# An encoder trunk on one Trainium2 core: a shorter stretch for preparing weight sums, and sums loaded into the activations' tiles

## The chip, the core and the metric

The kernel runs on one core of a Trainium2 chip. A core has TensorE (matrix multiply; the profile's PE, and PEld for its weight loads), VectorE (DVE), ScalarE (ACT), GpSimd (POOL) and SyncE (SP), whose queue issues nearly all transfers here, and 16 DMA engines that all queues share. The metric is the device time of one launch in microseconds (us); the time of a version is the median over its runs. The profile shows one execution.

## The reference

Two layers over 256 tokens of width 2048, in float32. Layer 0 mixes tokens with a bidirectional mLSTM, layer 1 with a bidirectional gated recurrence (HGRN2); each layer ends with a gated MLP with a convolution of width 3 over the tokens. Every stage has its RMS norm, and a last norm closes the trunk.

```python
for layer in range(DEPTH):
    hn = rmsnorm(h, norm_mix_g[layer])
    h = h + mixer(hn)                          # mLSTM, then HGRN2
    h = h + conv_glu(rmsnorm(h, norm_ffn_g[layer]), ffn_w_up[layer], ffn_conv_w[layer],
                     ffn_conv_b[layer], ffn_w_down[layer])
return rmsnorm(h, final_g)

def conv_glu(hn, w_up, conv_w, conv_b, w_down):
    a, v = jnp.split(hn @ w_up, 2, axis=-1)    # 2048 -> 2 x 5504
    c = conv_b + sum of the neighbours a[t-1], a[t], a[t+1] times conv_w
    return (gelu(c) * v) @ w_down              # 5504 -> 2048
```

The change lies in `conv_glu`, the feed-forward stage, of both layers.

## The kernel before

**Numbers in two parts.** Weights and activations are float32. Each piece of weights is split into a part `wh`, which ScalarE rounds to TensorE's type (L147), and the rest `wl`, which VectorE forms as weights minus `wh` (L148); activations likewise. A product is three matmuls (high by high, high by low, low by high); in the up projection two of them share one matmul of 512 columns (L357), and the third has 256 (L361).

**Stages of the feed-forward.** `ffn` (L1175) cuts the 43 blocks of 128 hidden columns into two parts, of 22 (`FA`) and 21 (`FB`). A part first has its **up chunks**, one for each block: 16 steps over the 2048 inputs, then `done_up` (L1189) makes the gated result on VectorE and ScalarE in a tile of the tag `avc`. Then follow two **pairs**, the down projection for two output column blocks of 512 each: `w0` for the left half of the output and `w1` for the right. So a layer runs: up chunks, two pairs, up chunks, two pairs. The input `x` of the up chunks lies in 16 tiles `xt0` to `xt15` of 512 columns for each partition (`Norm.take`, L404). Both parts read it. The next norm writes the same tiles anew, when the last pair is nearly through.

**Seven products instead of eight.** In a pair, `squares_by_seven` (L225) takes the hidden blocks two at a time, a **couple** (unit `u`), as a 2 x 2 square of matrices. For the couples in `SEVEN` it uses a scheme of Strassen's kind with seven products. For that it needs sums of weights: T1 to T4. T2, T3 and T4 lie in a tile T of 1536 columns. For most couples these sums are worked out in advance and kept in a scratch in DRAM (`tscr`); the few in `FLY` are made in place by `combine` (L202).

**Preparing sums.** `prepare` (L613) is a side job of a part's up chunks. For each of 12 couples it loads 2048 columns (two transfers of 512 KB on SP, L395), does four subtractions on VectorE (L632) and stores two halves to `tscr` (L635, two transfers of 512 KB). Side jobs run on a clock of the code's own: it ticks 0.65 at a time, 16 times in an up chunk, so a chunk is 10.4 units and a part is `nf * 10.4` (228.8 or 218.4). A job's `yield n` means that it isn't taken up again before n units have gone by; it is taken up at a tick. Before the change, the pause at the start is 18 and the period `(nf * 10.4 - 26) / 12`; within a period there are pauses of a half, four of a 24th, and a third. The tiles for this (`praw`) have the tags `wh` and `wl` of the pool `ff`, of two buffers each. The loads are in program order with the loads of up weights on SP (`late`, L394); the stores aren't.

**A pair's weights.** `split_squares` (L187) first waits, in the order of issue, until all that its pair needs has been prepared (`side.until`: what is left of the job is then issued at once). Then, a unit at a time, it loads 1536 columns of weights into a `raw` tile (three buffers, L135), and for a stored couple T into a tile of the tag `avc` (L198; three buffers, `TEMP`, the ones that `done_up` uses as well) and T1 into the rest of `raw` (L199). Each piece of 1024 columns is then split by L147 and L148. Every third piece uses tiles `wh` and `wl` of the pool `ff`. Pieces are fetched three ahead of TensorE (`LOOK`).

**What sets the order.** The queues of the engines work in order. The framework orders instructions for each engine by priority, the order of issue, and a simulated timeline; matmuls of the up chunks, and loads by `late`, are held in program order. A load waits on SP until its tile is free, and what stands behind it waits too.

**The end.** `FinalNorm` (L476) loads the final norm's weights into `xt0` to `xt3` (four tiles of 512 columns) ahead of the first pair of the last layer's second part, and uses `xt4` and `xt5` as work tiles.

Of the kernel before, what the change touches and what calls it, by code (L numbers as in the profile page):

```python
# [8 lines left out]
F32 = mybir.dt.float32  # L9
F32R = mybir.dt.float32r  # L10
# [5 lines left out]
P = 128  # L16
T = 256
D = 2048
KT = D // P
# [33 lines left out]
SPLIT = (0, 2, 5), (0, 2, 5)  # L53
END = 3
# [12 lines left out]
def trunk_kernel(ctx, tc, xT, x_d, fg_d, pp_d, cst_d, w_gate, w_first, w_aq, w_ak, w_av, w_ao, w_aout, w_ao2,  # L67
# [119 lines left out]
    def split_squares(ch, parts):  # L187

        units, raws, kept = (ch.nk + 1) // 2, {}, {}
        side.until(lambda: all(ch.waits))  # L190

        def raw(u):
            if u not in raws and u < units:
                n = 1536 if u in ch.stored else min(2048, 1024 * ch.nk - 2048 * u)
                raws[u] = load_raw(ch.src, 2048 * u, 2048 * u + n)
                if u in ch.stored:
                    kept[u] = temporary(ch.pool, "T")
                    nc.sync.dma_start(kept[u], ch.stored[u][:, 0:1536])  # L198
                    nc.sync.dma_start(raws[u][:, 1536:2048], ch.stored[u][:, 1536:2048])  # L199
            return raws.get(u)  # L200

        def combine(u):  # L202
            r, T = raw(u), temporary(ch.pool, "T")
            B11, B22, B21, B12 = (r[:, j * 512:(j + 1) * 512] for j in range(4))
            T2, T3, T4 = (T[:, j * 512:(j + 1) * 512] for j in range(3))
            for x, y, out in ((B12, B22, T3), (B12, B11, B12), (B22, B12, T2), (B21, T2, T4)):
                dve.tensor_tensor(out, x, y, ALU.subtract)
            kept[u] = T

        for u in range(units):  # L210
# [4 lines left out]
            if u in ch.seven:  # L215
                yield *parts(kept[u][:, 0:1024], 1024, more=ch.pool), 1
            if 2 * u + 1 < ch.nk:
                yield *parts(r[:, 1024:2048], 1024, more=ch.pool), 1
            if u in ch.seven:
                yield *parts(kept[u][:, 1024:1536], 512, more=ch.pool), 1  # L220
# [177 lines left out]
    class Norm:  # L398

        def __init__(self, gname, goff):  # L400
            self.g, self.o = gname, goff
            self.xs, self.rc_, self.R_ = [None] * KT, None, None

        def take(self, k, src, g=None, *pin):  # L404
            self.xs[k] = keep.tile([P, 2 * T], F32R, tag=f"xt{k}", name=f"xt{k}")
# [70 lines left out]
    class FinalNorm:  # L476
# [6 lines left out]
        def load(self):  # L483
            self.g = [keep.tile([P, 512], F32, tag=f"xt{c}", name=f"fg{c}") for c in range(4)]
# [20 lines left out]
        def half(self, ps, t):  # L505
# [5 lines left out]
            last = keep.tile([P, 512], F32, tag=f"xt{4 + t}", name="fl")  # L511
# [63 lines left out]
    def pair(src, nk, c0, x, sums, norm, seven):  # L575
# [34 lines left out]
        ch.stored, ch.waits, ch.pool, ch.ends, ch.rest = {}, (), None, False, False  # L610
# [564 lines left out]
    def ffn(layer, norm, nxt):  # L1175
# [40 lines left out]
        for part, (f0, nf) in enumerate(((0, FA), (FA, FB))):  # L1216
# [3 lines left out]
            def prep(todo=todo, finished=finished, nf=nf):  # L1220
                if not pairs[0].pool:
# [3 lines left out]
                                  todo, 18.0, (nf * 10.4 - 26.0) / len(todo), finished, late, True))  # L1225
# [6 lines left out]
            def two(src, c0, norm, seven, fly, shares, GT=GT, SX=SX, nf=nf):  # L1232
                ch = pair(src, nf, c0, lambda k: GT[k], lambda u: SX[u], norm, seven)
                ch.waits, left = [], [u for u in seven if u not in fly]
# [148 lines left out]
```

## Time and profile before

| | us |
|---|---|
| median of three runs | 2368.85 |
| the three runs | 2365.73, 2370.08, 2368.85 |
| the profiled execution | 2366.48 |
| its span, first to last instruction | 2364.5 |
| TensorE busy | 2354.1 |
| VectorE busy | 1993.5 |
| ScalarE busy | 1470.0 |

The feed-forward stages lie at these times in the profiled execution: layer 0 has up chunks from 388.7 to 634.3, pairs to 742.3, up chunks to 975.2 and pairs to 1080; layer 1 has up chunks from 1663.7 to 1909.4, pairs to 2017.5, up chunks to 2250.4 and pairs to 2356. The mean granted clock of TensorE is 0.999. Rows of the profile name an instruction by its line (L148), engine, operation and tiles (out<-in); "idle before" is time in which the engine stood still ahead of it, and the arrow names what ended that. A window row gives the stretch, its length, the busy time of every engine with the number of instructions, the clock, the DMA engines' share, and GB/s.

### The profile page before, as it was taken

Reading aid. Unit: us, or ns where it says so; the run is one execution under the profiler, and the core shown is the slowest. Engines: PE = TensorE matmul, PEld = TensorE weight load, DVE = VectorE, ACT = ScalarE, POOL = GpSimd, SP = SyncE. Lnnn points to the kernel's source line nnn. Section 1 sums busy time; section 2 is a strip of 40 time slices with the busy share of each in tenths; the row PEclk is TensorE's granted clock in tenths of the full one; section 3 lists DMA queues with packets and bytes.
Section 4 is the critical chain, followed back from the end, with each engine's and each line's share of the span. In section 5 each row is a group of like instructions: output and inputs, shape, how many; then the busy total and the mean of one; then the engine's idle time right before and its main releaser. Section 6 shows DMA issues by size and latency. Waiting matters only on the chain. (4 is left out here: it accounts for less than half of the span.)

```text
span 2364.5 us, 38407 instructions
## 1 busy us (share of the span) xinstructions
PE 2354.1 (100%) x14545; PEld 2016.2 (85%) x14545; DVE 1993.5 (84%) x3087; ACT 1470.0 (62%) x2340; POOL 196.5 (8%) x244
## 2 busy tenths in 40 slices
PE   9999999999999999999999999999999999999998
PEld 8888888888888888888888888888888888888887
DVE  7777687888998898897888888778789889888888
ACT  7655456555665555676777777776555567455565
POOL 0100000000000000000232322220000000000000
PEclk9999999999999999999999999999999999999999
DMA  8776656888888878996556665646788888888896
GB/s 303 239 248 242 213 195 211 295 282 292 313 321 327 306 282 292 330 334 230 208 203 223 212 225 204 214 169 228 270 300 289 289 321 335 295 287 302 309 351 221
DMA packets 122266, 632.97 MB, mean 268 GB/s; under 512 B 13776, under 2 KB 14928, under 8 KB 77664
## 3 DMA queue, kind: packets, MB, share of 16 engines
q1 hardware_dynamic: 120384, 626.51, 75.0%
q0 software_dynamic: 1120, 3.21, 0.8%
q8 instruction: 114, 1.87, 0.3%
q10 hardware_dynamic: 576, 0.79, 0.1%
q14 instruction: 72, 0.59, 0.1%
HBM read 562.24 MB, written 68.22 MB: 267 GB/s over the span
## 5 line engine op out<-in xcount | busy, mean ns | idle before, releaser
L357 PE MATMUL mm<-xt,wh 128*128 128x512 f32 x3776 | 1312.0, 394 | 0.0
L148 DVE TENSOR_TENSOR wl<-raw,wh 128x1024 fp32r<-128x1024 f32 (+1 forms) x844 | 1037.3, 1234 | 222.6 <-ACT wh L147 214.5
L147 ACT CAST wh<-raw 128x1024 fp32r<-128x1024 f32 (+1 forms) x844 | 875.3, 1042 | 513.0 <-PE mm L357 305.8
L361 PE MATMUL mm<-xt,wl 128*128 128x256 f32 x3776 | 1043.5, 278 | 0.0
L357 PEld LDWEIGHTS mm<-xt,wh 128*128 128x128 f32 x3776 | 705.6, 188 | 160.6 <-issue 0.4
L361 PEld LDWEIGHTS mm<-xt,wl 128*128 128x128 f32 x3776 | 709.4, 188 | 4.5
L373 PE MATMUL mm<-wh,xt 128*128 128x512 f32 x1024 | 324.4, 392 | 0.6 <-ACT wh L147 0.5
L236 PE MATMUL pc<-wh,g 128*128 128x512 f32 (+1 forms) x716 | 243.2, 388 | 0.3 <-ACT wh L147 0.2
L373 PEld LDWEIGHTS mm<-wh,xt 128*128 128x128 f32 x1024 | 191.2, 188 | 40.0 <-ACT wh L147 1.1
L632 DVE TENSOR_TENSOR praw<-praw 128x512 f32<-128x512 f32 x252 | 174.1, 691 | 44.7 <-DMA praw<-in_w_d 29.0
L373 PE MATMUL mm<-wl,xt 128*128 128x512 f32 x512 | 199.7, 391 | 0.0
L236 PEld LDWEIGHTS pc<-wh,g 128*128 128x128 f32 x716 | 134.1, 188 | 29.0 <-ACT wh L147 1.5
L236 PE MATMUL mm<-wh,sx 128*128 128x512 f32 x432 | 153.4, 389 | 0.0
L148 DVE TENSOR_TENSOR wl<-T,wh 128x1024 fp32r<-128x1024 f32 (+1 forms) x144 | 135.9, 955 | 13.3 <-ACT wh L147 8.9
L147 ACT CAST wh<-T 128x1024 fp32r<-128x1024 f32 (+1 forms) x144 | 118.6, 835 | 44.7 <-DMA T<-tscr 18.2
L236 PE MATMUL pc<-wl,g 128*128 128x512 f32 (+1 forms) x358 | 138.8, 388 | 0.0
L591 POOL TENSOR_TENSOR hm<-hm,u 128x512 f32<-128x512 f32 x10 | 14.8, 1481 | 1223.8 <-DVE u L590 1223.8
L373 PEld LDWEIGHTS mm<-wl,xt 128*128 128x128 f32 x512 | 96.2, 188 | 18.6
L1071 DVE TENSOR_TENSOR QK<-QK,G 128x256 f32<-128x256 f32 x224 | 104.6, 515 | 6.2 <-ACT kq L1050 5.9
L1195 ACT COPY avc<-mm 128x256 f32<-128x256 f32 x172 | 64.0, 372 | 63.9 <-PE mm L361 63.6
L1050 ACT COPY kq<-QK 128x512 f32<-128x512 f32 x112 | 74.5, 669 | 37.3 <-DVE QK L1071 29.5
L236 PEld LDWEIGHTS mm<-wh,sx 128*128 128x128 f32 x432 | 81.0, 188 | 16.9 <-ACT wh L147 0.2
(246 smaller groups left out, 2263.1 us busy)
## 6 DMA issues: line engine op xcount, KB each, us to landing
raw<-in_w_up SPq DMA_DIRECT2D x172, 1024.0 KB, 6.1
tscr<-praw SPq DMA_DIRECT2D x126, 512.0 KB, 6.7
praw<-in_w_d SPq DMA_DIRECT2D x120, 512.0 KB, 6.8
raw<-in_w_bq SPq DMA_DIRECT2D x48, 1024.0 KB, 5.0
T<-tscr SPq DMA_DIRECT2D x63, 768.0 KB, 7.6
raw<-in_w_d SPq DMA_DIRECT2D x60, 768.0 KB, 6.0
raw<-in_w_ao SPq DMA_DIRECT2D x24, 1024.0 KB, 4.8
raw<-in_w_d SPq DMA_DIRECT2D x24, 1024.0 KB, 7.7
```

The source lines that it names most:

```text
L147: pin(act.copy(wh[:, :m], r))
L148: pin(dve.tensor_tensor(wl[:, :m], r, wh[:, :m].bitcast(F32), ALU.subtract))
L236: pin(pe.matmul(ps, a, b, start=bank not in begun, stop=stop and i == 2))
L357: hold(pe.matmul(ps[f], wh[:, c:c + P], x, start=k + kk == 0, stop=False))
L361: hold(pe.matmul(ps[f][:, 0:T], wl[:, c:c + P], x[:, 0:T], start=False, stop=k + kk == ch.nk - 1))
L373: pe.matmul(ps[t], x[:, a + t * P:a + (t + 1) * P], w[:, c], start=st and i == 0, stop=sp and i == 2)
L591: pool.tensor_tensor(part(1, 0), part(1, 0), u, ALU.add)
L632: dve.tensor_tensor(out, x, y, ALU.subtract)
L1050: act.copy(m, blocks(QK, h))
L1071: dve.tensor_tensor(two[:, j], two[:, j], by[:, j], ALU.mult)
L1195: act.copy(z, p[:, T:2 * T])
```

## The change

- The period of `prepare` in a part's up chunks becomes `(nf * 10.4 - 60) / 12` instead of `(nf * 10.4 - 26) / 12`. The number of couples and their instructions stay.
- In the pairs of each layer's second part, the couples 2, 3 and 4 get their T not in a tile of the tag `avc` but in tiles of `x`: T2 and T3 (1024 columns) in one tile, T4 (512 columns) in half of another. `LENT` gives for each couple the tile, the other tile and its half. A stored couple's T comes then in two transfers (512 KB and 256 KB) instead of one of 768 KB.
- For that the 16 tiles of `x` are joined by twos into eight (`xt0` to `xt7`) of 1024 columns. The final norm's weights lie in two such tiles, its work tile in a third.

```diff
--- before.py
+++ after.py
@@ -51,6 +51,7 @@
 FLY = (2,), (5,), (2,), ()
 FIRST = 6
 SPLIT = (0, 2, 5), (0, 2, 5)
+LENT = {2: (3, 4, 0), 3: (5, 4, 1), 4: (6, 7, 0)}
 END = 3
 SCRATCH = 4096
 SEVEN_MIX = (2, 4, 6)
@@ -186,26 +187,36 @@
 
     def split_squares(ch, parts):
 
-        units, raws, kept = (ch.nk + 1) // 2, {}, {}
+        units, raws, kept, halves = (ch.nk + 1) // 2, {}, {}, {}
         side.until(lambda: all(ch.waits))
+
+        def place(u):
+            if u not in ch.lent:
+                T = temporary(ch.pool, "T")
+                return T[:, 0:1024], T[:, 1024:1536], T
+            i, j, h = ch.lent[u]
+            if j not in halves:
+                halves[j] = keep.tile([P, 1024], F32, tag=f"xt{j}", name="T")
+            return keep.tile([P, 1024], F32, tag=f"xt{i}", name="T"), halves[j][:, h * 512:(h + 1) * 512], None
 
         def raw(u):
             if u not in raws and u < units:
                 n = 1536 if u in ch.stored else min(2048, 1024 * ch.nk - 2048 * u)
                 raws[u] = load_raw(ch.src, 2048 * u, 2048 * u + n)
                 if u in ch.stored:
-                    kept[u] = temporary(ch.pool, "T")
-                    nc.sync.dma_start(kept[u], ch.stored[u][:, 0:1536])
+                    kept[u] = place(u)
+                    for T, a, b in [(kept[u][2], 0, 1536)] if kept[u][2] else zip(kept[u], (0, 1024), (1024, 1536)):
+                        nc.sync.dma_start(T, ch.stored[u][:, a:b])
                     nc.sync.dma_start(raws[u][:, 1536:2048], ch.stored[u][:, 1536:2048])
             return raws.get(u)
 
         def combine(u):
-            r, T = raw(u), temporary(ch.pool, "T")
+            r, (T, T4, _) = raw(u), place(u)
             B11, B22, B21, B12 = (r[:, j * 512:(j + 1) * 512] for j in range(4))
-            T2, T3, T4 = (T[:, j * 512:(j + 1) * 512] for j in range(3))
+            T2, T3 = (T[:, j * 512:(j + 1) * 512] for j in range(2))
             for x, y, out in ((B12, B22, T3), (B12, B11, B12), (B22, B12, T2), (B21, T2, T4)):
                 dve.tensor_tensor(out, x, y, ALU.subtract)
-            kept[u] = T
+            kept[u] = T, T4
 
         for u in range(units):
             r = raw(u)
@@ -213,11 +224,11 @@
             if u + 1 in ch.seven and u + 1 not in ch.stored:
                 combine(u + 1)
             if u in ch.seven:
-                yield *parts(kept[u][:, 0:1024], 1024, more=ch.pool), 1
+                yield *parts(kept[u][0], 1024, more=ch.pool), 1
             if 2 * u + 1 < ch.nk:
                 yield *parts(r[:, 1024:2048], 1024, more=ch.pool), 1
             if u in ch.seven:
-                yield *parts(kept[u][:, 1024:1536], 512, more=ch.pool), 1
+                yield *parts(kept[u][1], 512, more=ch.pool), 1
 
     def banks():
         return [psm.tile([P, 512], F32, tag="mm", name="mm") for _ in range(2)]
@@ -399,10 +410,12 @@
 
         def __init__(self, gname, goff):
             self.g, self.o = gname, goff
-            self.xs, self.rc_, self.R_ = [None] * KT, None, None
+            self.xs, self.two, self.rc_, self.R_ = [None] * KT, {}, None, None
 
         def take(self, k, src, g=None, *pin):
-            self.xs[k] = keep.tile([P, 2 * T], F32R, tag=f"xt{k}", name=f"xt{k}")
+            if k // 2 not in self.two:
+                self.two[k // 2] = keep.tile([P, 4 * T], F32R, tag=f"xt{k // 2}", name=f"xt{k // 2}")
+            self.xs[k] = self.two[k // 2][:, k % 2 * 2 * T:(k % 2 + 1) * 2 * T]
             split(self.xs[k], src, col(self.g, self.o + k) if g is None else g, *pin)
 
         def squares(self, c, pin=lambda ins: ins):
@@ -481,7 +494,9 @@
             self.rc = small[:, 8:10]
 
         def load(self):
-            self.g = [keep.tile([P, 512], F32, tag=f"xt{c}", name=f"fg{c}") for c in range(4)]
+            g = [keep.tile([P, 1024], F32, tag=f"xt{c}", name=f"fg{c}") for c in range(3)]
+            self.g = [g[c // 2][:, c % 2 * 512:(c % 2 + 1) * 512] for c in range(4)]
+            self.last = g[2]
             for c in range(4):
                 pool.dma_start(self.g[c], fg_d[:, c * 512:(c + 1) * 512].broadcast_to([P, 512]))
 
@@ -508,7 +523,7 @@
             dve.tensor_tensor(hm[:, t, 1024:1536], hm[:, t, 1024:1536], ps[0], ALU.add)
             square(hm[:, t, 1024:1536], ss[:, 2:3])
             dve.tensor_scalar(rc, ss[:, 2:3], 1.0 / D, rc, ALU.mult, ALU.add)
-            last = keep.tile([P, 512], F32, tag=f"xt{4 + t}", name="fl")
+            last = self.last[:, 512 * t:512 * t + 512]
             h = hm[:, t, 1536:2048]
             dve.tensor_tensor(h, h, ps[1], ALU.add)
             m = 256 if t else 512
@@ -607,7 +622,7 @@
 
         ch = Chunk("st", src, nk, x, done)
         ch.mid, ch.seven, ch.sums = mid, seven, sums
-        ch.stored, ch.waits, ch.pool, ch.ends, ch.rest = {}, (), None, False, False
+        ch.stored, ch.waits, ch.pool, ch.ends, ch.rest, ch.lent = {}, (), None, False, False, {}
         return ch
 
     def prepare(tiles, todo, first, period, finished, start, ahead):
@@ -1222,7 +1237,7 @@
                     begin()
                 side.push(prepare(lambda i: [box["mp"].tile([P, 1024], F32, tag=("wh", "wl")[i % 2], bufs=MORE, name="praw")
                                              for _ in range(2)],
-                                  todo, 18.0, (nf * 10.4 - 26.0) / len(todo), finished, late, True))
+                                  todo, 18.0, (nf * 10.4 - 60.0) / len(todo), finished, late, True))
 
             for i in range(nf):
                 chunks.append(Chunk("fm", w_up[layer, f0 + i], KT, norm.x, done_up(f0 + i, i, GT, SX, SEVEN[layer][part]),
@@ -1231,6 +1246,8 @@
                                     fixed=part + i > 0))
             def two(src, c0, norm, seven, fly, shares, GT=GT, SX=SX, nf=nf):
                 ch = pair(src, nf, c0, lambda k: GT[k], lambda u: SX[u], norm, seven)
+                if part:
+                    ch.lent = LENT
                 ch.waits, left = [], [u for u in seven if u not in fly]
                 for n, (todo, finished) in zip(shares, [early[layer]] + lists):
                     for u in left[:n]:
```

## Prediction

> **What bounds the kernel now.** I read the page's engine table first, then a window for each of the four up stretches and the four stretches of pairs, then what the weight loads of TensorE (PEld) waited for, and last the instructions around the longest wait.
>
> ```profile
> PE 2354.1 (100%) x14545; PEld 2016.2 (85%) x14545; DVE 1993.5 (84%) x3087; ACT 1470.0 (62%) x2340; POOL 196.5 (8%) x244
> ```
>
> ```profile
> 388.70:634.30 245.60, 245.60 (x1422) 214.86 (x1421) 213.91 (x349) 141.22 (x223) 0.70 (x1) 1.00 0.85 294
> 634.30:742.30 108.00, 107.93 (x477) 89.01 (x476) 99.39 (x112) 73.08 (x86) 3.54 (x2) 1.00 0.86 320
> 742.30:975.20 232.90, 232.90 (x1346) 203.68 (x1345) 202.47 (x324) 128.30 (x200) 3.53 (x2) 1.00 0.85 301
> 975.20:1080.00 104.80, 104.80 (x471) 86.79 (x470) 97.93 (x111) 74.53 (x96) 7.01 (x4) 1.00 0.82 299
> 1663.70:1909.40 245.70, 245.70 (x1422) 214.85 (x1422) 211.32 (x345) 139.90 (x221) 0.70 (x1) 1.00 0.84 292
> 1909.40:2017.50 108.10, 107.88 (x476) 88.86 (x475) 102.59 (x117) 73.13 (x87) 3.71 (x3) 1.00 0.88 325
> 2017.50:2250.40 232.90, 232.90 (x1346) 203.68 (x1345) 202.44 (x317) 127.17 (x198) 5.63 (x6) 1.00 0.86 302
> 2250.40:2356.00 105.60, 105.07 (x475) 86.76 (x475) 92.61 (x109) 69.84 (x89) 7.58 (x5) 1.00 0.78 290
> ```
>
> The columns are the stretch and its length, the busy time of PE, PEld, DVE, ACT and POOL, the granted clock, the DMA share and GB/s. Odd rows are the up chunks of one part, even rows its two pairs. TensorE is busy through all eight: 1382.78 of 1383.60 us. That alone doesn't exclude slow matmuls, so the pace is read too. The two steady stretches of up chunks while couples are being prepared give 200.00 / 1156 = 173.0 ns and 185.00 / 1069 = 173.1 ns between matmuls:
>
> ```profile
> 412.00:612.00 200.00, 200.00 (x1156) 174.90 (x1155) 175.34 (x288) 112.33 (x179) 0.00 (x0) 1.00 0.84 290
> 612.00:634.30 22.30, 22.30 (x131) 19.52 (x130) 20.76 (x34) 14.27 (x22) 0.00 (x0) 1.00 1.01 369
> 765.00:950.00 185.00, 185.00 (x1069) 161.81 (x1068) 159.49 (x261) 103.28 (x164) 0.00 (x0) 1.00 0.84 297
> 950.00:975.20 25.20, 25.20 (x147) 22.03 (x147) 23.47 (x39) 14.04 (x22) 0.00 (x0) 1.00 0.95 337
> 2250.40:2303.00 52.60, 52.07 (x229) 42.34 (x229) 43.64 (x49) 36.28 (x44) 4.45 (x2) 1.00 0.95 360
> ```
>
> No matmul is added or removed, so the floor stays. What the change can win is the time in which TensorE waits in the pairs. All waits of the weight loads there, first in the first part's pairs (630 to 742 us), then in the third's (1905 to 2020), then in the fourth's (2245 to 2357); in the second's there is none (us in total, times, longest):
>
> ```profile
> PEld pc L236 <- ACT wh L147: 0.5, 1, 0.5
> ...
> PEld pc L236 <- ACT wh L147: 0.7, 1, 0.7
> PEld mm L236 <- ACT wh L147: 0.2, 1, 0.2
> ...
> PEld mm L236 <- DVE wl L148: 1.0, 1, 1.0
> PEld pc L236 <- ACT wh L147: 0.4, 1, 0.4
> PEld mm L236 <- ACT wh L147: 0.2, 1, 0.2
> ```
>
> Together 3.0 us. The most that can be won in the changed stages is **3.0 us**, 0.13% of the time; 0.2% (4.7 us), about what a measurement of this kernel can tell from no change, isn't there to be had in these waits.
>
> The longest of them lies 10 us into the last part's first pair:
>
> ```profile
> 2255.05 0.33 SPq L135 DMA_DIRECT2D raw<-in_w_d  x1
> 2255.43 0.43 SPq L198 DMA_DIRECT2D T<-tscr  x1
> ...
> 2260.31 0.39 PE L236 MATMUL pc<-wh,g 128*128 128x512 f32 x1
> ...
> 2260.54 0.49 PE L236 MATMUL mm<-wh,g 128*128 128x512 f32 x1
> 2260.86 0.40 PE L236 MATMUL pc<-wh,g 128*128 128x512 f32 x1
> 2261.34 1.05 ACT L147 CAST wh<-T 128x1024 fp32r<-128x1024 f32 x1 [0.56 <-DMA T<-tscr]
> ...
> 2261.79 0.50 PE L236 MATMUL mm<-wl,g 128*128 128x512 f32 x1 [0.53 <-DVE wl L148]
> 2262.13 0.40 PE L236 MATMUL mm<-wh,g 128*128 128x512 f32 x1
> ```
>
> Undisturbed starts lie 0.23 us apart (2260.31 to 2260.54). From 2260.86 to 2261.79 it is 0.93, a loss of 0.70; the steps before and after it (0.32 and 0.34) lose 0.1 each. A few matmuls on, the next wait (0.38 us of PEld) is the last 0.2. I put this knot at **1.1 us**. Its sums T were asked for at 2255.43 and taken up at 2261.34. They were asked for late, because T has to have one of three buffers that the up chunks' results (avc) hold, and the last chunks' results are still being made then.
>
> **The change part by part.**
>
> *The shorter stretch.* The rows of L632 give the cost of a couple and when it is done:
>
> ```profile
> L632 DVE TENSOR_TENSOR praw<-praw 128x512 f32<-128x512 f32 x40 | 27.4, 685 | 3.9 <-issue 2.9 <-DMA praw<-in_w_d 0.9
> L632 DVE TENSOR_TENSOR praw<-praw x48: 680/684/694, 406.5 to 623.5; 128x512 f32<-128x512 f32 x48
> L632 DVE TENSOR_TENSOR praw<-praw x48: 679/683/695, 758.3 to 964.0; 128x512 f32<-128x512 f32 x48
> ```
>
> The first row is the stretch 412 to 612: 40 subtractions, so 10 couples in 200 us, 20 us each, 2.74 us of VectorE each. The code's period is (228.8 - 26) / 12 = 16.9 of its own time units, but every one of its six pauses is rounded up to ticks of 0.65: 8.45 + 4 x 1.3 + 5.85 = 19.5, and 12 of these and the first 18 make 252, more than the 228.8 that the part has. So before, the last two couples were not paced at all but were issued at once when the first pair asked for its weights; the window 612 to 634.3 shows it as a DMA share of 1.01. After: 14.07 becomes 7.15 + 4 x 0.65 + 5.2 = 14.95; 12 of them and 18.2 are 197.6, which is 31 units or three up chunks ahead of the pairs, not four (for the second part 14.3, 190 of 218.4, again under three). One unit is 245.6 / 228.8 = 1.073 us, so a couple comes every 16.0 us instead of 20, in the second part every 15.3.
>
> What each instruction of the moved step costs: 48 subtractions a part, unchanged in number, at 685 ns. Without them VectorE is busy (175.34 - 27.4) / 200 = 0.74; with one couple in 16.0 us 0.91 instead of 0.88, in the second part about 0.92. That hides behind TensorE as it does now: in the unpaced bursts VectorE ran at 20.76 of 22.30 and 23.47 of 25.20 us (0.93) and TensorE didn't wait in either. 24 loads and 24 stores a part, on SP's queue: 4 x 512 KB a couple, 2.1 MB, is 105 GB/s at 20 us, 131 at 16.0 and 137 at 15.3. So the up chunks go from 290 to 316 GB/s and from 297 to about 327, by the share 0.84 to about 0.92. Transfers in this window:
>
> ```profile
> raw<-in_w_up SPq DMA_DIRECT2D x36, 1024.0 KB, 6.0
> tscr<-praw SPq DMA_DIRECT2D x20, 512.0 KB, 6.4
> praw<-in_w_d SPq DMA_DIRECT2D x20, 512.0 KB, 7.0
> ```
>
> A raw tile lasts 245.6 / 44 = 5.6 us of TensorE and there are three, so a new one has two such times, 11 us, to land; it takes 6.0. The loads of couples stand in program order ahead of raw loads on SP, and wait for the stores of the couple two before, whose 6.4 us fit into the 12 units between them. I cost it at 0; the ends are -0.5 (below) and +20 (first rival). What is freed: no couples' traffic in the last three up chunks, when the pairs' first loads are issued, and no unpaced burst on VectorE ahead of the last chunk's results. Of the waits in the first and third part (0.5 and 0.9 us, ends 0 and all 1.4 gone) I count none as won. Where the third part's is, a piece waits for T although the couples had been subtracted 30 us before (last start 1899.7):
>
> ```profile
> L632 DVE TENSOR_TENSOR praw<-praw x48: 679/684/693, 1681.5 to 1899.7; 128x512 f32<-128x512 f32 x48
> ...
> 1929.28 1.05 ACT L147 CAST wh<-T 128x1024 fp32r<-128x1024 f32 x1 [3.36 <-DMA T<-tscr]
> ```
>
> *The lent tiles.* In both pairs of each second part, T2 and T3 of couples 2, 3 and 4 go to tiles of x, T4 to half of another. All are stored ones: 12 loads of 768 KB become 12 of 512 and 12 of 256 KB. The added 12 issues hold SP 0.33 us each (the raw row at 2255.05), 1 us a pair, spread over 52 us. x's tiles are read last by the last up chunk, the first of them at half of it: about 2250.4 - 5.6 = 2244.8, the last at 2250.4. T of couple 2 may so be asked for up to 9 us earlier than 2255.43, and nothing that stands behind it on SP is held longer than now: the raw load ahead of it waited to 2255.05 anyway. The 1.1 us knot goes; next in line are couple 5 and later, which then find all three avc buffers free. Value **-1.1**, ends -1.6 (all PEld waits of that part) and 0.
>
> By the Trainium skill, "DMA: Bandwidth & Descriptors", section Bandwidth / Measured, transfers should be batched to 1 MiB or more, which speaks against cutting one into two. Its fit of 2.0 us a transfer beside the bytes gives, as an estimate from that page, 12 x 2.0 = 24 us more DMA time, 2392 us if all of it were exposed; that a small transfer costs nearly as much as a large one the trace confirms (6.8 and 7.6 us, in a rival below).
>
> *x in eight tiles instead of sixteen, and the final norm's rows in halves of two of these.* No instruction changes, and x's tiles were always written in twos. A false wait between the two halves would show at a norm's start; bounds 0 and 4 norms x 0.5 us (one split by ACT is 0.51 us):
>
> ```profile
> 4.53 0.51 ACT L379 ACTIVATE xt<-gx 128x256 fp32r<-128x256 f32 x1 [1.58 <-DMA gx<-in_xT]
> ```
>
> I take 0, since the second half is written right behind the first, before the matmuls are issued.
>
> *Sum.* The profiled execution took 2366.48 us (span 2364.5 and 2.0 around it); 2366.48 - 1.1 = 2365.4. The three runs' median is 2.37 us above that execution. I forecast for the median: 2368.85 - 1.1 = **2367.7 us**, no change by 0.2%.
>
> **The rivals.**
>
> *Denser transfers starve the up chunks (slower).* Place: the 180 us in which couples are now prepared, four times. Up chunks with couples ran at 290 to 302 GB/s so far; nobody has asked 316 to 327 of them for 180 us. TensorE has up to three pieces ready, 3 x 245.6 / 88 = 8.4 us. If the stretch carried only 300 of 322 GB/s, it would end 180 x 22 / 300 = 13 us late, 4.8 beyond what is ready; four times, 19 us: 2387 us. It decides below about 322 x 180 / 189 = 307 GB/s. Against it: the last row of the windows above, 360 GB/s for 52.6 us with 0.5 us of waiting, and 369 GB/s with none. Chance 0.14.
>
> By the Trainium skill, the same page, section "Where 436 GB/s comes from", transfers between HBM and SBUF are held to about 358 GB/s by the HBM side. The trace has gone beyond it (369), and the demand here lies below either.
>
> *The cut transfers land late (slower).* A 256 KB load needs almost as long as a 768 KB one when the pairs begin:
>
> ```profile
> T<-tscr SPq DMA_DIRECT2D x3, 768.0 KB, 7.6
> raw<-tscr SPq DMA_DIRECT2D x4, 256.0 KB, 6.8
> ```
>
> If two halves took turns they would need up to 14 us, 6 more, and one such delay in each of four pairs is 24 us less the 9 us head start of two of them, about +6 to +15: 2374 to 2383. Against it: they overlap on the same 16 engines, and T4 is needed last in its unit. Chance 0.04.
>
> *It doesn't do what it says.* SP keeps T of couple 2 behind the raw load that waits to 2255.05, so the head start isn't used, or another piece is late instead: 2368.9. Chance 0.25, and the same verdict as mine.
>
> *More is won than the profile shows.* The three runs lie up to 3.6 us above the profiled one (2370.08). If that is made of longer waits of the same kind, and the change removes them with all 3.0 us, the median falls to 2368.85 - 2.4 - 3.0 = 2363.5. Chance 0.12.
>
> **How the numbers follow.** My forecast holds 0.45, the change without effect 0.25: no change 0.70. Slower 0.14 + 0.04 = 0.18, faster 0.12. The likeliest case alone reaches from 2365.0 to 2370.5, by the runs' own spread. To leave out no more than 2 in 10, the range takes in the gain of the last rival and the mild end of the slower ones: 2363.3 to 2374.
>
> **What would show it.** Right: L632 ends some 25 us ahead of each first pair; the window ahead of the pairs loses its DMA share of 1.01 and 0.95; T for couples 2 to 4 is asked for before the second parts' pairs begin, and no wait is left near 2261; 173 ns between matmuls in the up chunks. Wrong: waits of ACT for raw<-in_w_up, which aren't in this profile, weight loads waiting on L357, or VectorE above 0.95 between two up chunks.

## The result and the profile after

| | median, us | runs | lowest to highest |
|---|---|---|---|
| before | 2366.95 | 8 | 2365.26 to 2370.08 |
| after | 2376.49 | 8 | 2370.28 to 2379.09 |

The ratio is **1.0033, 95% interval 1.0024 to 1.0042**: slower by a third of a per cent (the medians themselves lie 9.5 us apart, 0.40%). The forecast was no change, at 2367.7 us. The profiled execution of the changed kernel took 2377.22 us, its span 2375.2 us, 10.7 more than the span of before. Lines after the change stand 11 to 15 lower down in the code: L148 and L149 split the weights, L247 is the pairs' product, L368 and L372 are the up chunks' two matmuls, L647 is the couples' subtraction, L209 loads T.

What TensorE's weight loads waited for, over the whole run of the changed kernel (us in total, times, longest):

```profile
PEld mm L372 <- DVE wl L149: 4.1, 3, 1.8
PEld pc L247 <- DVE wl L149: 2.1, 1, 2.1
PEld mm L247 <- ACT wh L148: 1.9, 2, 1.3
PEld pc L247 <- ACT wh L148: 1.4, 3, 0.6
...
PEld mm L247 <- DVE wl L149: 1.1, 2, 0.8
```

The first row is new: 4.1 us in the up chunks, which had none. The pairs (L247) have 6.5 us where they had 3.0. Of these, 5.2 lie in the fourth part. Together that is 7.6 us more than before. Another 1.6 us follow from a lower clock, shown below, so 9.2 of the 10.7 us are accounted for by these rows. Counted from matmul to matmul, the up chunks of the first and the third part take 1.1 and 3.8 us longer than before, the fourth part's pairs with the end 5.1, and all the rest 0.7.

**The up chunks.** The longest of the three waits is this one, in layer 1's first part (timeline of the changed kernel):

```profile
1859.03 0.69 DVE L647 TENSOR_TENSOR praw<-praw 128x512 f32<-128x512 f32 x1 [3.88 <-DMA praw<-in_w_d]
...
1859.63 0.48 DVE L1217 SCALAR_TENSOR_TENSOR avc<-avc,pp 128x255 f32<-128x255 f32 x1
...
1860.03 0.68 DVE L647 TENSOR_TENSOR praw<-praw 128x512 f32<-128x512 f32 x1
1860.20 0.42 ACT L1218 ACTIVATE avc<-avc 128x256 f32<-128x256 f32 x1 [5.01 <-DVE avc L1217]
1860.63 1.22 DVE L149 TENSOR_TENSOR wl<-raw,wh 128x1024 fp32r<-128x1024 f32 x1
...
1861.90 0.39 PE L372 MATMUL mm<-xt,wl 128*128 128x256 f32 x1 [1.49 <-DVE wl L149]
```

VectorE stands still for 3.88 us before a subtraction whose couple hasn't landed. It works in order, so the last chunk's result (L1217) and the next piece of weights (L149) wait behind it, and TensorE waits for that piece. The couple itself is wanted by nobody for 50 us. How short the lead of such a load is can be seen in layer 0's first part, first after, then before:

```profile
570.84 1.36 SPq L406 DMA_DIRECT2D praw<-in_w_d  x2
...
580.53 0.69 DVE L647 TENSOR_TENSOR praw<-praw 128x512 f32<-128x512 f32 x1 [3.40 <-DMA praw<-in_w_d]
```

```profile
598.61 0.80 SPq L395 DMA_DIRECT2D praw<-in_w_d  x2
...
606.15 0.69 DVE L632 TENSOR_TENSOR praw<-praw 128x512 f32<-128x512 f32 x1
```

Before, VectorE came to the subtraction 7.5 us after the load was issued and found it just landed. After, it stood free 6.3 us after the issue and waited the other 3.4. Over the whole run the median time of a praw load to land rose from 6.8 to 7.7 us. VectorE waited for such loads before, too; the whole-run rows are, before and after:

```profile
DVE praw L632 <- DMA praw<-in_w_d: 29.0, 22, 3.4
```

```profile
DVE praw L647 <- DMA praw<-in_w_d: 40.7, 27, 3.9
```

The transfers themselves went as worked out. In the stretch with couples the share is 0.88 at 310 GB/s (0.92 and 316 had been estimated), and ScalarE's waits for up weights, of which there were none, come to 1.5 us (three, the longest 0.9) and lie at 596, 864 and 1837, not where TensorE waits.

```profile
412.00:588.00 176.00, 175.18 (x1011) 153.00 (x1010) 152.53 (x252) 94.59 (x153) 0.00 (x0) 1.00 0.88 310
588.00:636.00 48.00, 48.00 (x279) 42.30 (x278) 43.18 (x70) 30.86 (x49) 0.00 (x0) 1.00 0.76 259
2300.00:2303.20 3.20, 3.20 (x8) 2.53 (x9) 3.20 (x4) 2.37 (x3) 1.55 (x1) 0.50 0.47 136
```

The second row is the quiet time ahead of the pairs that the shorter stretch leaves (couples end at 586.1; 1.01 had been the share here). The third row belongs to the next point.

**The fourth part's pairs.** These start at about 2256 in the changed kernel, and the knot of 1.1 us is gone. New waits come at 2285 and 2297. The last of them, in the timeline:

```profile
2298.61 2.35 DVE L149 TENSOR_TENSOR wl<-raw,wh 128x1024 fp32r<-128x1024 f32 x2
2299.43 2.00 ACT L148 CAST wh<-raw 128x1024 fp32r<-128x1024 f32 x2 [1.96 <-DMA raw<-in_w_d]
...
2299.89 0.76 PE L247 MATMUL pc<-wl,g 128*128 128x512 f32 x1 [1.62 <-DVE wl L149]
2300.45 0.63 PE L247 MATMUL pc<-wh,g 128*128 128x512 f32 x1
```

Now it is `raw`, the weights themselves, that is late. The transfers issued from 2243 to 2300, most of the first pair:

```profile
T<-tscr SPq DMA_DIRECT2D x7, 768.0 KB, 9.2
raw<-in_w_d SPq DMA_DIRECT2D x6, 768.0 KB, 10.0
T<-tscr SPq DMA_DIRECT2D x6, 512.0 KB, 11.4
```

A pair has three lent couples, so three transfers of 512 KB. Six were issued: the second pair's lent sums (3 x 768 KB, 2.4 MB) were fetched during the first, which runs to about 2313. The raw loads take 10.0 us to land; before, seven of them in this place took 6.8. The queue on SP has filled up as well. Its waits from 2250 to 2285 are:

```profile
SPq L209 <- DMA T<-tscr: 6.4, 8, 1.6
SPq L209 <- DMA raw<-in_w_d: 4.0, 2, 2.3
SPq L136 <- DVE wl L149: 2.8, 3, 1.8
SPq L209 <- DMA raw<-tscr: 2.5, 2, 1.3
SPq L136 <- DMA T<-tscr: 2.4, 2, 1.5
```

Issues wait there for the landing of earlier transfers: from 2255.99 to 2282.04, each of 19 issues in a row comes within 0.12 us of the landing of the transfer that SP had issued eight before. Raw loads (L136) stand behind sums that aren't needed for 30 us. In the kernel before, SP waited in this place only for tiles that VectorE was still reading or writing.

After the wait of 2 us the matmuls run at half pace: the window 2300 to 2303.2 above has a granted clock of 0.50. The half clock lasts from 2299.95 to 2303.36, and the eight matmuls in it start about 427 ns apart instead of 227, which is the 1.6 us more.

### The profile page after: what moved, and what is told of

It is laid out like the page before. It is cut to its first block, busy times and chain, and to the rows that moved or that the text cites. A ratio compares the mean times of both kernels' runs of the same rounds, so it can differ in the third digit from the quotient of the medians.

```text
span 2375.2 us, 38403 instructions
## 1 busy us (share of the span) xinstructions
PE 2358.8 (99%) x14545; PEld 2018.3 (85%) x14545; DVE 1990.2 (84%) x3087; ACT 1470.5 (62%) x2340; POOL 196.5 (8%) x244
## 5 line engine op out<-in xcount | busy, mean ns | idle before, releaser
L368 PE MATMUL mm<-xt,wh 128*128 128x512 f32 x3776 | 1313.6, 394 | 0.0
L149 DVE TENSOR_TENSOR wl<-raw,wh 128x1024 fp32r<-128x1024 f32 (+1 forms) x844 | 1037.7, 1235 | 217.0 <-ACT wh L148 211.1
L148 ACT CAST wh<-raw 128x1024 fp32r<-128x1024 f32 (+1 forms) x844 | 875.7, 1043 | 494.0 <-PE mm L368 279.5
L372 PE MATMUL mm<-xt,wl 128*128 128x256 f32 x3776 | 1045.1, 278 | 3.1 <-DVE wl L149 3.1
L368 PEld LDWEIGHTS mm<-xt,wh 128*128 128x128 f32 x3776 | 705.6, 188 | 160.9 <-issue 0.4
L372 PEld LDWEIGHTS mm<-xt,wl 128*128 128x128 f32 x3776 | 709.7, 188 | 8.6 <-DVE wl L149 4.1
L247 PE MATMUL pc<-wh,g 128*128 128x512 f32 (+1 forms) x716 | 244.4, 390 | 0.2 <-ACT wh L148 0.2
L647 DVE TENSOR_TENSOR praw<-praw 128x512 f32<-128x512 f32 x252 | 174.2, 691 | 56.7 <-DMA praw<-in_w_d 40.7
L247 PEld LDWEIGHTS pc<-wh,g 128*128 128x128 f32 x716 | 134.6, 189 | 29.0 <-ACT wh L148 1.4
L247 PE MATMUL mm<-wh,sx 128*128 128x512 f32 x432 | 153.4, 389 | 0.2 <-ACT wh L148 0.2
L149 DVE TENSOR_TENSOR wl<-T,wh 128x1024 fp32r<-128x1024 f32 (+1 forms) x144 | 136.3, 960 | 13.9 <-ACT wh L148 13.3
L148 ACT CAST wh<-T 128x1024 fp32r<-128x1024 f32 (+1 forms) x144 | 118.3, 834 | 43.5 <-PE pc L247 16.9
L247 PE MATMUL pc<-wl,g 128*128 128x512 f32 (+1 forms) x358 | 139.7, 390 | 1.6 <-DVE wl L149 1.6
L247 PEld LDWEIGHTS mm<-wh,sx 128*128 128x128 f32 x432 | 81.0, 188 | 17.4 <-ACT wh L148 0.7
```

Of the source, the lines that this page charges most:

```text
L148: pin(act.copy(wh[:, :m], r))
L149: pin(dve.tensor_tensor(wl[:, :m], r, wh[:, :m].bitcast(F32), ALU.subtract))
L247: pin(pe.matmul(ps, a, b, start=bank not in begun, stop=stop and i == 2))
L368: hold(pe.matmul(ps[f], wh[:, c:c + P], x, start=k + kk == 0, stop=False))
L372: hold(pe.matmul(ps[f][:, 0:T], wl[:, c:c + P], x[:, 0:T], start=False, stop=k + kk == ch.nk - 1))
```

## The experiments

Two theories stood from here on. **Mine:** two separate causes, the subtractions that wait in VectorE's queue for a late couple, and the second pair's lent sums ahead of the first pair's weights. **Rivals:** the denser traffic as such; the transfers cut in two; the first pair's lent transfers.

| run | us | before beside it | ratio, 95% interval |
|---|---|---|---|
| e1 shorter period alone | 2369.81 | 2367.93 | 1.0006 (0.9997 to 1.0015) |
| e2 lent tiles, old period | 2371.35 | 2367.93 | 1.0014 (1.0005 to 1.0023) |
| e3 shorter period, lent in first pairs | 2368.60 | 2367.93 | 1.0002 (0.9993 to 1.0011) |
| e4 all T cut in two | 2367.27 | 2367.93 | 0.9996 (0.9987 to 1.0005) |
| e5 couples' loads on GpSimd's queue | 2377.83 | 2367.19 | 1.0047 (1.0035 to 1.0060) |
| e6 the same, lent in first pairs | 2376.23 | 2367.19 | 1.0041 (1.0028 to 1.0055) |
| e7 shorter period, lent in second pairs | 2377.44 | 2367.19 | 1.0044 (1.0031 to 1.0056) |
| e8 old period, lent in first pairs | 2364.85 | 2367.19 | 0.9988 (0.9980 to 0.9997) |
| e9 as e2, pairs' loads in program order | 2372.55 | 2367.25 | 1.0021 (1.0012 to 1.0030) |
| e10 as e3, couples' loads earlier | 2365.61 | 2367.25 | 0.9993 (0.9984 to 1.0001) |
| e11 changed kernel with both repairs | 2369.14 | 2367.25 | 1.0007 (0.9998 to 1.0016) |
| e12 x in eight tiles alone | 2368.50 | 2367.25 | 1.0006 (0.9997 to 1.0014) |

### e1: the shorter period alone

```diff
 # the kernel before
-                                  todo, 18.0, (nf * 10.4 - 26.0) / len(todo), finished, late, True))
+                                  todo, 18.0, (nf * 10.4 - 60.0) / len(todo), finished, late, True))
```

> The kernel before with the shorter period alone. My theory has two separate causes, and this run holds only the first: in the up chunks a couple's subtraction stands in VectorE's queue before its load has landed, and the wl pieces behind it wait with it. Then VectorE's wait for praw should rise from 29.0 us to about 40 us, TensorE should wait for wl in the up chunks (about 4 us in all, at two to four places, as in the changed kernel: 1.0, 1.1 and 1.8 us), and the time should be about 2 to 4 us above before. The pairs of the fourth part should show no wait above 1.2 us. Rival 1, the transfers cut in two or lent are the only cause: no time lost, 0 us. Rival 2, the up weights themselves come late because of the denser traffic: the same loss, but ScalarE waits for raw<-in_w_up.

Measured 1.0006. What TensorE waited for, beside the start:

```profile
PE mm L361 <- DVE wl L148: 2.1, 3, 1.0
```

Three waits in the up chunks, at the places where the changed kernel has them (near 582, 1843 and 1861). ScalarE's waits for up weights are two, 1.4 us in all, and not at these places. The wait for praw rose to 54.3 us. The interval takes in no change, so it is the trace that shows this cause and not the time: the up chunks of the first and the third part take 1.7 and 2.4 us longer than before.

In the fourth part's pairs (2245 to 2365) no weight load waits at all. The knot of 1.1 us is gone with the shorter stretch alone, though nothing is lent here, and the pairs with the end take 1.2 us less than before. That is part of why the time shows less than the up chunks lose.

### e2: the lent tiles alone

```diff
 # the changed kernel
-                                  todo, 18.0, (nf * 10.4 - 60.0) / len(todo), finished, late, True))
+                                  todo, 18.0, (nf * 10.4 - 26.0) / len(todo), finished, late, True))
```

> The changed kernel with the old period. It holds the lent tiles and not the shorter stretch. My theory: the fourth part's pairs still lose 4 to 6 us, since the second pair's six lent transfers (of 4096 and 2048 bytes a partition) are issued during the first pair, ahead of its own weights; no wait in the up chunks; the 1.1 us knot of before is gone; 3 to 6 us above before. Rival, the loss in the pairs comes from the stretch (couples' stores or loads in another place): no loss here, -1 us.

Measured 1.0014, 3.4 us. The waits of the weight loads in the fourth part's pairs (2245 to 2365):

```profile
PEld mm L247 <- ACT wh L148: 3.7, 4, 1.2
PEld pc L247 <- DVE wl L149: 1.4, 2, 0.9
PEld pc L247 <- ACT wh L148: 0.6, 1, 0.6
```

5.7 us, as in the changed kernel (5.2), and none in the up chunks. So the two causes are separate. A wait at 2261 is still there, against what was expected, though e8 below, with the same period, hasn't it; which order of loads brings it back wasn't traced further.

### e3 and e7: lent tiles in the first or the second pair only

```diff
 # the changed kernel; e7 has c0 == 2
-                if part:
+                if part and c0 == 0:
                     ch.lent = LENT
```

> The changed kernel, but only the first pair of each second part gets lent tiles. My theory: the second pair's sums wait for avc tiles again, so they can't be fetched early, and the 6 us in the fourth part's pairs go; the up chunks keep their 4 us; about 1.5 to 4 us above before, 4 to 6 below the changed kernel. Rival, the first pair's own lent transfers (or their being cut) push its weights back: the loss in the pairs stays, 8 us above before.

> The changed kernel with lent tiles in the second pair of each second part only. My theory: the second pair's lent sums need not wait for the first pair's reading of the tiles, so they are fetched as early or earlier, and the fourth part's first pair loses at least what it loses in the changed kernel (4 us or more, and the 1.1 us knot back); 6 to 10 us above before. Rival, the loss comes from the first pair's lent transfers: no loss there beyond 1.2 us; 2 to 4 us above before.

Measured 1.0002 for the first pair only and 1.0044 for the second only. The fourth part's pairs have these waits, e3 first, then e7:

```profile
PEld pc L247 <- DVE wl L149: 0.2, 1, 0.2
```

```profile
PEld mm L247 <- ACT wh L148: 5.7, 1, 5.7
PEld pc L247 <- ACT wh L148: 0.4, 1, 0.4
PEld pc L247 <- DVE wl L149: 0.2, 1, 0.2
```

In e7 the first pair has no lent tile, so every transfer of 512 KB is of the second pair; those issued from 2238 to 2264, when the first pair had hardly begun:

```profile
raw<-in_w_d SPq DMA_DIRECT2D x4, 768.0 KB, 9.2
T<-tscr SPq DMA_DIRECT2D x4, 768.0 KB, 9.8
T<-tscr SPq DMA_DIRECT2D x3, 512.0 KB, 11.4
```

All three had been issued nearly 60 us before their pair starts, at about 2311. TensorE then waited 5.7 us at one go, for a T of the first pair that was issued at 2260.71 and landed at 2269.88. So lending in the second pair costs, and lending in the first pair costs nothing there. That it also takes the knot away e3 can't show, since the shorter stretch does that by itself (e1); e8 below has the old period.

In layer 0's second part (975 to 1085), where the same tiles are lent, the cost is smaller: its weight loads don't wait at all in the changed kernel, 1.6 us in e2 and 2.6 us in e7. In the changed kernel SP waits there (971 to 1006) for tiles alone and never for a landing. What makes the two parts differ wasn't tested; the final norm's weights (1 MB on GpSimd's queue) are loaded in the last part only.

### e4: every T cut in two

```diff
 # the kernel before
-                    nc.sync.dma_start(kept[u], ch.stored[u][:, 0:1536])
+                    for a, b in ((0, 1024), (1024, 1536)):
+                        nc.sync.dma_start(kept[u][:, a:b], ch.stored[u][:, a:b])
```

> The kernel before with every stored couple's T fetched in two transfers (1024 and 512 columns), in all pairs: 63 more transfers instead of 12. My theory: 0 to +1 us, no new wait above 1 us in any pair. Rival, cutting them costs (my prediction's second rival): with five times as many cuts, more than +4 us, and TensorE waits in several pairs for T.

Measured 0.9996: 63 cut transfers cost nothing that can be measured, which drops the prediction's second rival.

### e8: the old period and lent tiles in the first pair

```diff
 # the changed kernel: the period of e2 and the condition of e3 together
```

> Lent tiles for the first pair of each second part only, and the old period. My theory: neither of the two losses, and T of couples 2 to 4 early enough for the knot of before to go: no wait above 0.8 us in the fourth part's pairs and none in the up chunks; 0 to 1.5 us below before. Rival, lending as such costs, or the last couples' burst still delays the first pair: 1 us or more above before.

Measured 0.9988 (0.9980 to 0.9997), 2.3 us below the medians beside it, and faster than both kernels. Its eleven runs lie between 2364.07 and 2365.96. The fourth part's pairs have 0.2 us of waiting: with the old period too, lending in the first pair takes the knot away. DMA engines are as full as in the changed kernel and in e2, which differs from e8 only by lending in the second pair as well. Here are 2251 to 2290 of e8, then the same of e2, then 2257 to 2296 of the changed kernel:

```profile
2251.00:2290.00 39.00, 39.00 (x173) 32.28 (x172) 33.41 (x39) 28.71 (x37) 0.00 (x0) 1.00 1.00 389
```

```profile
2251.00:2290.00 39.00, 36.98 (x161) 29.39 (x160) 29.89 (x36) 25.22 (x33) 0.00 (x0) 1.00 1.03 408
```

```profile
2257.00:2296.00 39.00, 37.94 (x165) 30.48 (x165) 28.22 (x33) 23.72 (x30) 0.00 (x0) 1.00 1.02 394
```

The engines are full in all three, at 389, 408 and 394 GB/s, but TensorE is busy for all 39.00 us in e8, for 36.98 in e2 and for 37.94 in the changed kernel. Full engines alone aren't the cause, then. That it is which bytes go first is tested by e9.

### e5 and e6: couples' loads on another queue

```diff
 # the changed kernel; e6 has e3's condition as well
-                                  todo, 18.0, (nf * 10.4 - 60.0) / len(todo), finished, late, True))
+                                  todo, 18.0, (nf * 10.4 - 60.0) / len(todo), finished, nc.gpsimd.dma_start, True))
```

> The changed kernel with the couples' loads on GpSimd's queue, which has nothing else to do in the up chunks, instead of SP's, where they stand in program order behind the up weights' loads. Bytes and the shorter period stay. My theory: in the changed kernel a load is asked for only 8 to 11 us before its subtraction and lands up to 1.4 us before it or later; asked for where the job issues it, it lands earlier, VectorE's wait for praw falls from 40.7 us to below 15 us, and TensorE's 4 us of waits in the up chunks go; the fourth part's pairs keep their loss: 3 to 6 us above before. Rival, the denser traffic as such makes the loads late: the waits for praw stay at 40 us or more, and the up chunks keep their loss; 6 to 9 us above before.

> Couples' loads on GpSimd's queue and lent tiles for the first pair of each second part only, with the shorter period. If both causes are as I say, no wait of TensorE above 1.2 us is left in the feed-forward stages and the 1.1 us knot of before is gone: 0 to 2 us below before. Rival, one of the losses has another cause: 2 us or more above before.

Both times were missed by far (1.0047 and 1.0041). The mechanism came out half: TensorE's waits for wl in the up chunks went, at the same bytes, and VectorE's wait for praw fell to 10.6 us in e5. But loads that are no longer bound to the up weights' order were moved ahead, and with them the first subtractions, to where the norm is still being made. In e5 one stood there at 1672.89 after 4.90 us of idle time, with the norm's steps behind it; its load, issued at 1663.87, landed at 1672.8. TensorE waited for x instead (e5):

```profile
PE mm L368 <- DVE xt L391: 4.3, 4, 2.0
```

It is the same fault in another place. The same wait is in e6's profile, with 2.3 us. e6's five runs spread from 2368.46 to 2381.63 and its profile is of the fastest, so what its slow ones lost stays open.

### e10: couples' loads earlier on the same queue

```diff
 # e3
-            yield period / 2
             if ahead:
                 load(i + 1)
+            yield period / 2
```

> Lent tiles for the first pair only and the shorter period, as in the third experiment, but a couple's load is issued half a period (7.15 units, about 7.7 us) earlier on the same queue, at the same bytes. My theory: the loads then land before VectorE comes to their subtractions; VectorE's wait for praw falls from 58.4 us to below 15, no wait of TensorE for wl in the up chunks (3.0 and 1.4 us of lost pace there go); 0 to 2 us below before. Rival, the denser traffic itself: the waits stay above 40 us, 0.5 to 3 us above before. A further way for it to fail: the load then waits for the stores of the couple two before, and holds the up weights behind it on SP.

Measured 0.9993 (0.9984 to 1.0001), 1.6 us below the medians beside it; e3 had been 0.7 above. VectorE's wait, e3 then e10:

```profile
DVE praw L647 <- DMA praw<-in_w_d: 58.4, 34, 4.7
```

```profile
DVE praw L647 <- DMA praw<-in_w_d: 27.2, 27, 2.7
```

Not below 15 as expected, but the longest fell from 4.7 to 2.7 us, and no wait of TensorE in the up chunks is left. The length of VectorE's wait doesn't decide alone: one of 2.6 us near 1837 in e3 cost TensorE 0.65 us, one of 3.4 us near 847 in the kernel before cost nothing. The bytes and the queue are the same as in e3, and the couples even come closer together: from 412 to 569 e10 moves 329 GB/s, e3 315. So the denser traffic itself isn't the cause; when the loads are asked for is. This rests on the traces: the intervals of e3 and e10 overlap, and the profiled execution is one of the slowest of e3 and one of the fastest of e10.

### e9 and e11: the pairs' loads in program order

```diff
 # e2; e11 is the changed kernel with this and e10's edit
-                raws[u] = load_raw(ch.src, 2048 * u, 2048 * u + n)
+                raws[u] = load_raw(ch.src, 2048 * u, 2048 * u + n, late)
...
-                        nc.sync.dma_start(T, ch.stored[u][:, a:b])
+                        late(T, ch.stored[u][:, a:b])
...
-                    nc.sync.dma_start(raws[u][:, 1536:2048], ch.stored[u][:, 1536:2048])
+                    late(raws[u][:, 1536:2048], ch.stored[u][:, 1536:2048])
```

> Old period, lent tiles in both pairs as in the second experiment, but all loads of the pairs' weights and sums are issued on SP in program order, so that the second pair's lent sums can't be asked for ahead of the first pair's weights. My theory: the loss in the fourth part's pairs goes (at most 1.2 us of it is left), 0 to 2 us below the kernel before, 3 to 6 below the second experiment. Rival, what costs is not the place in the queue but lending in the second pair as such (for instance the tiles' reuse): 3 us or more above before. A further way for it to fail: program order makes raw loads wait behind a T that waits for its tile, with new waits in all pairs.

> The changed kernel with both repairs: the pairs' loads in program order, and the couples' loads half a period earlier. If the two causes are the whole loss, it lies 0 to 3 us below before and 8 us or more below the changed kernel. If a third cause is left, it lies above before.

Measured 1.0021 and 1.0007. In e9 the weight loads don't wait at all between 2245 and 2310, with lending in both pairs: the place in the queue was the cause there. But the further way to fail came true. Program order holds in all pairs, and those of layer 1's first part (1905 to 2022), where nothing is lent, now wait:

```profile
PEld pc L247 <- DVE wl L149: 2.7, 4, 1.0
PEld mm L247 <- ACT wh L148: 1.1, 2, 0.6
PEld mm L247 <- DVE wl L149: 0.9, 3, 0.4
PEld pc L247 <- DVE hm L613: 0.6, 2, 0.3
```

So e9 and e11 are a good test of the cause and a poor repair. By its expectation e11, above before, leaves a third cause, though its interval takes in no change. Its larger waits lie at other places than the changed kernel's, all in pairs: near 695, 1970 and 2347. Fixing the order is the likely one, as in e9, but it wasn't separated further.

### e12: the joined tiles alone

```diff
 # the changed kernel: the period of e2, and
-                if part:
-                    ch.lent = LENT
```

> x in eight tiles of 1024 columns instead of sixteen, nothing lent, old period. My theory: no difference, within 1 us of before, the knot of 1.1 us in the fourth part stays, since T of couple 2 still waits for an avc tile. Rival, the joined tiles alone change the order or the waits: more than 2 us either way.

Measured 1.0006 (0.9997 to 1.0014), no difference, with the knot in the fourth part still there. As predicted, the joined tiles cost nothing that can be told.

## Why the prediction was wrong

- **What bounds the kernel** held: TensorE's pace in the up chunks is nearly the same (175.18 us for 1011 matmuls, 173.3 ns each), and what changed is waiting and a short stretch at half clock. From that the prediction rightly saw how little could be won. It didn't ask as hard how much could be lost.
- **"I cost it at 0", the shorter stretch, failed.** The prediction priced the denser couples by averages: VectorE's share (0.91) and GB/s. Both came out lower (152.53 / 176.00 = 0.87, and 310 GB/s) and were harmless. The price lies in single waits: a subtraction in an in-order queue whose load was issued only 8 to 12 us ahead. In place of 0 the up chunks took 4.9 us longer in the profiled execution. The row that told of it, VectorE's 29.0 us in 22 waits for praw, stood in the profile before and wasn't used. It says that the loads were already arriving at the last moment. "Whose 6.4 us fit into the 12 units between them" was checked for the tiles and not for the subtraction. The first rival had the right stage and sign, but by the wrong mechanism: in no run does TensorE wait for up weights that landed late. ScalarE's waits for them, a sign that the prediction named, did appear, but only 1.5 us of them in the changed kernel and 9.5 in e5, and no wait of TensorE followed. e1 and e3 show the term in their traces (4.1 and 4.5 us in the up chunks), less in time (1.9 and 0.7 us in the medians, both intervals with no change in them), and in e10 it is gone.
- **The end "0" of the lent tiles failed.** The knot that the value -1.1 stood for is gone in the changed kernel, as forecast, and e8 shows that lending in the first pair is enough for that. But e1 shows that the shorter stretch is enough as well, which the prediction hadn't seen, and with lending in both pairs alone (e2) waits in the same place remain; so that this part came out is partly luck. The upper end was wrong. "Nothing that stands behind it on SP is held longer than now" looked at the first pair's tiles only. In the second pair the lent tiles have no one to wait for but the first pair's reading of them, or nobody at all (e7), so the wait for an avc buffer, which had kept these loads back, was gone for them as well. 2.4 MB then went ahead of the weights in a stretch whose DMA engines were full. In place of -1.1 the fourth part's pairs with the end took 5.1 us longer than before. Against e8, whose pairs don't wait, lending in the second pair costs 4.7 us in e2, 6.1 in the changed kernel and 7.3 in e7; in the last two that includes a stretch at half clock.
- **The cut transfers at 0** held (e4), and so did **x in eight tiles at 0** (e12).
- **"Three up chunks ahead of the pairs, not four" failed**, harmlessly. The subtractions of the first part end at 586.1 and its pairs start at about 636, 50 us or over four chunks. The ticks were counted rightly, but the job's clock is that of the order of issue, which runs ahead of TensorE (pieces are fetched three ahead), and the framework places the job's steps as early as it can. That is read from the code; no run separates the two.
- **The range** (to 2374.0) was too narrow, since both terms that failed had been given an upper end of 0 outside the rivals.

The lengths of the stages in the profiled executions put the two causes side by side (us, from matmul to matmul: from the first unbroken stretch of a part's up chunks to its pairs, and from the fourth part's pairs to the end of the span):

| | up chunks, first part | up chunks, third part | pairs of the fourth part, and the end |
|---|---|---|---|
| before | 236.4 | 236.4 | 114.2 |
| after | 237.5 | 240.2 | 119.3 |
| e1 shorter period alone | 238.1 | 238.8 | 113.0 |
| e2 lent tiles, old period | 236.4 | 236.4 | 117.9 |
| e7 shorter period, lent in second pairs | 236.7 | 238.8 | 120.5 |
| e8 old period, lent in first pairs | 236.4 | 236.4 | 113.2 |
| e10 shorter period, lent in first pairs, earlier loads | 236.4 | 236.4 | 113.2 |

The two causes alone, 1.0006 and 1.0014, come to less than the change's 1.0033. In the profiled executions the changed kernel loses 0.8 us more in the up chunks than e1, and has a half-clock stretch that e2 hasn't. Why these come out longer together wasn't tested.

## What to carry to other kernels

Ahead of making a side job denser, look up how long its loads lie ahead of their first use on an in-order engine, and what that engine already waits for them: a job that nobody needs soon stops everything behind it. A buffer that is short also holds loads back; whoever lends more space should say which loads it lets go first, and give it only to those that are needed next. Here the two together were the difference between a loss of 0.3% (the changed kernel) and no loss that can be told (e10).

## What the runs showed of the hardware

A wait of TensorE can cost more than its length. After the wait of 2.0 us at 2298 the granted clock was 0.50 for 3.4 us, and 512-column matmuls started 427 ns apart instead of 227. It isn't the length alone that decides: in e3 a wait of 2.4 us in the up chunks (at 1858) left the clock at 1.00, and in e5 one of 2.0 us at 2300 did too, while another of 2.3 us at 1676 brought it down from 1679.1 to 1685.9:

```profile
1681.00:1686.00 5.00, 5.00 (x16) 4.23 (x17) 2.98 (x6) 1.46 (x3) 1.10 (x2) 0.51 0.99 330
```

In each of these traces the granted clock changes only at whole steps of 3.413 us from its first rise: after 672, 673 and 693 steps in the changed kernel, after 490, 492 and 693 in e5. What went with the outcome is how long TensorE stood still within one such step. After steps in which it was idle for a share of 0.54 (the changed kernel), 0.58 (e5) and 1.00 (e7, at half clock from 2270.6 to 2274.0) the clock was halved; after steps with 0.44 (the changed kernel, the wait at 1860), 0.47 (e3) and 0.48 (e5, the wait at 2300) it wasn't. These are few cases, and the ends of matmuls in a profile are modelled.

The Trainium skill, "TensorE: Matmul & The Clock Gate", section "Part 1: The HAM clock gate", explains such a drop by a free-running window of about 3.4 us in which the array was idle. The steps of 3.413 us agree with these windows; that a window idle for a share of 0.54 is enough is less than the page has.

SP's issues waited for the landing of earlier transfers once eight of its own were on the way (rows of SP above): of the 848 in the changed kernel's trace none comes before the transfer issued eight before it has landed. Transfers that are asked for too early take such places. Whether that is a limit of the queue or of the semaphores that the framework hands out, the trace doesn't tell.
